# A hybrid decoder layer on one core: value products that begin with the mask made last, and a new written order of the mix's stages

## The chip, the core and the metric

The kernel runs on one core of one Trainium2 chip. The metric is the device time of one execution in microseconds (us). Before the change it is 2168.46 us, the median of 3 runs (2168.17 to 2171.48).

Engine names are those of the profile: PE is the matmul engine, PEld its weight loads, DVE the vector engine, ACT the scalar engine, POOL the GpSimd engine, SP the engine that issues most DMAs.

## What is computed

One decoder layer over 2048 tokens of width 1024, in float32: two head groups side by side (the "mix"), then a gated MLP with a short convolution, then a final norm. Cut to what the change touches:

```python
u = rmsnorm(h, norm_mix_w)
proj = u @ w_in
hq, hf, hi, hg, att = split(proj)
o_hg = hgrn2_chunkwise(q_hg, k_hg, v_hg, log_f)          # 4 heads of 128, recurrent
o_hg = rmsnorm(o_hg, hg_norm_w) * silu(hg)
scores = where(band, q . k / 8, -inf)                    # 8 query heads of 64, 2 key/value heads
m = maximum(max(scores), sink)
p = exp(scores - m)
denom = sum(p) + exp(sink - m)
o_att = (p / denom) . v                                  # own block of 128 keys and the one before
h = h + concat(o_hg, o_att) @ w_out
h = h + (silu(conv(v @ w_gate)) * (v @ w_up)) @ w_down
out = rmsnorm(h, final_norm_w)
```

## The kernel before

The 2048 tokens go through in two halves of 1024. In each half the mix comes first (four recurrent heads in `hgrn`, four pairs of attention heads in `attend`), then the output projection (`out_proj`), the MLP's two up projections (`gate_up`) and its down projection (`down`). Large products are done in a split form: each float32 operand is a rounded part and a rest (`hi`, `lo`), and three matmuls of 512 columns make one product (L202 for the mix's projections).

**Stages.** `hgrn` and `attend` are generators: each `yield` ends a stage. The list `ORDER` names the stages one after the other, and the loop at the end of `hymba_layer` takes them in that order. For head n: `f`, `q` are the forget and query projections, `l` the seven levels of the chunk recurrence, `s` the states, `p` the output, `g` the gate projection, `w` the loading of its weights, `m` a split of a finished piece of the mix. For attention pair n: `qa` is its query projection, `sc` scores and softmax, `pv` and `pw` the value products of the first and the second 512 tokens. `v` is a value projection for two heads. The written order is not the last word: the kernel is built with a scheduler, which places each engine's instructions within their dependences, starting from that written order. What then stands on each engine is shown below, from the built programs.

**Matmuls of the mix, by their line.** L202 projections (results f, hq, q, g and, in `out_proj`, pop); L618 to L620 the value projection (pvv); L387 scores (psc); L423 transposes of the softmax (ppt); L434 value products (poT); L474 diagonal blocks (pdiag); L505 the five fine levels and L519 the two coarse ones (both plev); L552 transposes of K (pkn), L559 state updates (pu), L578 and L580 the head's output (po), L593 its transposes (pot). A row of the trace names the array that a matmul uses: 128\*128 is the whole array. L434 and L474 use half of its columns (128\*64), L519 a quarter or half (128\*32, 128\*64): the result has only 64 or 32 rows. Two products that use different halves of the columns can stand in the array at the same time. A float32 product at full precision (L434, L474, L505, L519, L559, L578, L580) has two records in the trace, a projection or a transpose one.

**The value products.** For each pair and each 512 tokens DVE makes four masked copies of the transposed softmax (L426), in this order: own block for key head 0, previous block for key head 0, own for key head 1, previous for key head 1 (tiles po, pp, po, pp). Then 16 products (L434, 14 at the very start of the sequence, where a block has no previous one) add up in one PSUM bank, poT: for each of four query blocks own and previous mask times V, for key head 0 (lower half of the columns) and key head 1 (upper half).

**Other names.** L512, L522 and L523 multiply Q and K by forget factors (F and a number) between the levels (DVE); L530 puts a level's result into ST (DVE); L404, L405 and L414 belong to the softmax (DVE), the last scales it; L214 splits a finished piece of the mix (DVE); L553 copies transposed K out of PSUM (ACT); L444 and L445 split the last pair's result into XH (ACT) and XL (DVE); L183 and L184 split loaded weights (ACT, DVE). In `hgrn` the flag `late` is set where `ORDER` has head n's `p` ahead of its `g`: then the gate is multiplied in behind the output (L491, L492, L595) and not before (L597).

Of the kernel before, what the change touches and what calls it, by code (L numbers as in the profile page):

```python
# [36 lines left out]
            ("P7", "S3", "T3"), ("P2", "A12", "B21"), ("P4", "A22", "T4")]  # L37
AFTER = {2: 'po'}
UP_AFTER = 'T2'
ORDER = ("f0 q0 l0 qa0 v0 s0 sc0 w0 pv0 p0 f1 q1 l1 g0 pw0 w1 qa1 g1 sc1 f2 s1 q2 p1 qa2 m0 pv1 pw1 l2 v1 "  # L40
         "s2 sc2 f3 m5 q3 g2 p2 pv2 pw2 qa3 m6 m1 sc3 l3 m4 m2 s3 g3 pv3 p3 pw3").split()
LEVELS = [1, 2, 4, 8, 16, 32, 64]
NEG = -1.0e30
UT = 7
# [5 lines left out]
def hymba_layer(ctx: ExitStack, tc: tile.TileContext, a: dict, out: bass.AP, rows_out: bass.AP):  # L50
# [18 lines left out]
    def ps(kind, name):  # L69
        return spaces[kind].tile([P, 512], F32, tag=kind, name=name)  # L70
# [3 lines left out]
    def halves():  # L74
        return [(b, slice(b * 512, (b + 1) * 512)) for b in range(NB)]
# [111 lines left out]
    def unit(src, X, name, order=range(KT), kind="mm", then={}, in_turn=False):  # L187


        hi, lo = src if isinstance(src, tuple) else prep(src)  # L190
        o = [ps(aux[b] if kind == "aux" else kind, f"{name}{b}") for b in range(NB)]
        order = list(order)
        for both in [[h] for h in halves()] if in_turn else [halves()]:
            for i, kt in enumerate(order):
                if i in then:
                    then[i]()
                wh, wl = hi[:, kt * P:(kt + 1) * P], lo[:, kt * P:(kt + 1) * P]
                xh, xl = X[kt]
                for w, x, f, l in ((wh, xh, kt == order[0], False), (wh, xl, False, False),
                                   (wl, xh, False, kt == order[-1])):  # L200
                    for b, bs in both:
                        nc.tensor.matmul(o[b], w, x[:, bs], start=f, stop=l)  # L202
        return o

    def new_x():
        return (xp.tile([P, HALF], F32R, tag="xh", name="XH", bufs=KT),
                xp.tile([P, HALF], F32R, tag="xl", name="XL", bufs=KT))
# [56 lines left out]
    def slot(name):  # L264
        return hp.tile([P, HALF], F32, tag="m", name=name, bufs=KT)
# [47 lines left out]
    def blocks(t, turn=False):  # L313

        v = t.rearrange("p (g r) -> p g r", r=32)
        return v[:, :, ::-1] if turn else v
# [6 lines left out]
    def rows(kv):  # L323
        return slice(kv * HD, (kv + 1) * HD)
# [32 lines left out]
    def attend(hf, j, X, invb, KS, V, mix, p):  # L357

        o = unit(a["w_att"][j], X, "q")
        qT = slot(f"att{j}")  # L360
        for b, bs in halves():
            nc.vector.scalar_tensor_tensor(blocks(qT[:, bs], b), blocks(o[b]), 0.125, blocks(invb[:, bs]),
                                           op0=ALU.mult, op1=ALU.mult)
            nc.scalar.activation(qT[:, bs], qT[:, bs], AF.Identity, bias=C.bq[:, j:j + 1])
        yield
        scs = []
        for g in range(NB):
            sc = p.tile([P, 2, 4, P], F32, tag="sc", name="sc", bufs=2)
            gs = slice(g * 512, (g + 1) * 512)
            for kv in range(2):  # L370
                r, other = rows(kv), rows(1 - kv)

                qh, ql = [p.tile([P, 512], F32R, tag="pp", name=n, bufs=4) for n in ("qh", "ql")]
                nc.scalar.copy(qh[r], qT[r, gs])
                nc.scalar.copy(qh[other], qT[r, gs])
                nc.vector.tensor_tensor(ql[r], qT[r, gs], qh[r].bitcast(F32), op=ALU.subtract)
                nc.scalar.copy(ql[other], ql[r].bitcast(F32))
                for i0 in (0, 2):
                    pb = ps("at", "psc")
                    first = hf == 0 and g == 0 and i0 == 0  # L380
                    for i in range(2):
                        n = g * 4 + i0 + i
                        w0 = 1 if first and i == 0 else 0
                        o = pb[:, i * 256 + w0 * P:(i + 1) * 256]
                        ks = slice((n + w0) * P, (n + 2) * P)
                        for t, qx in enumerate((qh, ql)):
                            nc.tensor.matmul(o, qx[:, (i0 + i) * P:(i0 + i + 1) * P], KS[:, kv, ks],  # L387
                                             start=t == 0, stop=t == 1)
                    pv = pb.rearrange("p (i w k) -> p i w k", i=2, w=2)
                    dst = sc[:, kv, i0:i0 + 2]  # L390
                    if first:
                        nc.vector.memset(dst[:, 0], NEG)
                        nc.scalar.copy(dst[:, 1], pv[:, 1, 0])
                    else:
                        nc.scalar.copy(dst, pv[:, :, 0])
                    nc.vector.copy_predicated(
                        dst, C.own.bitcast(U32).unsqueeze(1).to_broadcast([P, 2, P]), pv[:, :, 1])
            m = p.tile([P, 2, 4], F32, tag="mx", name="m", bufs=2)
            nc.vector.tensor_reduce(m.rearrange("p a b -> p (a b)"),
                                    sc.rearrange("p a b c -> p (a b) c"), axis=AX.X, op=ALU.max)  # L400
            sk = C.sinkb[:, j].unsqueeze(2).to_broadcast([P, 2, 4])
            nc.vector.tensor_tensor(m, m, sk, op=ALU.max)
            es = p.tile([P, 2, 4], F32, tag="es", name="es", bufs=2)
            nc.vector.tensor_tensor(es, sk, m, op=ALU.subtract)  # L404
            nc.vector.tensor_scalar(m, m, -1.0, None, op0=ALU.mult)  # L405
            den = p.tile([P, 2, 4], F32, tag="den", name="den", bufs=2)
            for kv in range(2):
                for i in range(4):
                    nc.scalar.activation(sc[:, kv, i], sc[:, kv, i], AF.Exp, bias=m[:, kv, i:i + 1],
                                         accum_out=den[:, kv, i:i + 1])  # L410
            nc.scalar.activation(es, es, AF.Exp)
            nc.vector.tensor_tensor(den, den, es, op=ALU.add)
            nc.vector.reciprocal(den, den)
            nc.vector.tensor_tensor(sc, sc, den.unsqueeze(3).to_broadcast([P, 2, 4, P]), op=ALU.mult)  # L414
            scs.append(sc)
        yield
        for g, sc in enumerate(scs):
            pm = []
            for kv in range(2):
                pm.append([p.tile([P, 4, P], F32, tag="pp", name=n, bufs=4) for n in ("po", "pp")])  # L420
                pt = ps("at", "ppt")
                for i in range(4):
                    nc.tensor.transpose(pt[:, i * P:(i + 1) * P], sc[:, kv, i], ident)  # L423
                ptv = pt.rearrange("p (i q) -> p i q", i=4)
                for dst, mk in zip(pm[kv], (C.ownT, C.prevT)):
                    nc.vector.tensor_tensor(dst, ptv, mk.unsqueeze(1).to_broadcast([P, 4, P]), op=ALU.mult)  # L426
            oT = ps("at", "poT")
            for i in range(4):
                n = g * 4 + i
                noprev = hf == 0 and n == 0  # L430
                for prev in range(1 if noprev else 2):
                    for kv in range(2):
                        r = rows(kv)
                        nc.tensor.matmul(oT[r, i * P:(i + 1) * P], V[:, n + 1 - prev, r], pm[kv][prev][:, i],  # L434
                                         start=prev == 0, stop=noprev or prev == 1)
            gs = slice(g * 512, (g + 1) * 512)
            if j < ATT_J - 1:
                nc.scalar.copy(qT[:, gs], oT)
                mix[4 + j] = qT
            else:  # L440
                if g == 0:
                    mix[4 + j] = new_x()
                h, l = mix[4 + j]
                nc.scalar.copy(h[:, gs], oT)  # L444
                nc.vector.tensor_tensor(l[:, gs], oT, h[:, gs].bitcast(F32), op=ALU.subtract)  # L445
            yield

    def hgrn(hf, h, X, invb, vs, WG, gates, mix, p, fu=None):
# [31 lines left out]

        late = ORDER.index(f"p{h}") < ORDER.index(f"g{h}")

# [605 lines left out]
    kv = [first_unit(X, W, i) for i in range(2)]  # L1088
    constants()
    xs.inverse("x")  # L1090
    f0 = unit(a["w_f"][0], X, "f", kind="aux", then={4: xs.spread})
    nxt = X, kv, xs.acc, xs.rs, f0
    for hf in range(NH):
        X, kv, invb, rs, f0 = nxt
        with ExitStack() as st:
# [6 lines left out]
            pairs = [attend(hf, h, X, invb, KS, V, mix, p) for h in range(HG)]  # L1102
            for name in ORDER:
                stage, n = name[:-1], int(name[-1])
# [87 lines left out]
```

## Time and profile before

| What | us |
|---|---|
| median of 3 runs | 2168.46 |
| the profiled execution, its own time | 2167.45 |
| span of the profiled execution (first to last instruction) | 2165.7 |
| mix of the first half, from the first attention projection to the unbroken run of the output projection | 46.7 to 397.0 of the span |
| mix of the second half | 1124.0 to 1471.0 |
| ACT busy in the span | 1046.9 (48%) |
| DVE busy in the span | 1624.0 (75%) |

The span is 1.75 us shorter than the profiled execution's own time, which counts what lies before the first and after the last instruction. The rows of the trace give start and length of each instruction in us from the start of the span. Matmuls overlap: a row of 512 columns lasts 0.39 us, but the next starts 0.23 us later. So the time that a piece of work takes on PE is read from the distance between starts, not from the lengths. In the timeline a row with x2 is two records that follow each other, and its length reaches from the start of the first to the end of the last.

### The profile page before, as it was taken

To read this page: it belongs to the slowest core of one execution; us is meant where nothing else is said; L and a number is where in the kernel's file an instruction comes from. 1 tells how busy PE (TensorE), PEld (TensorE's weight loads), DVE (VectorE), ACT (ScalarE), POOL (GpSimd) and SP (SyncE) were. 2 spreads that over 40 slices of the span, in tenths; PEclk is the share of its full clock that TensorE was granted. 3 is DMA by queue.
4 is the path that set the end of the run, shared out by engine and by line. 5 is a ranking of instruction groups with operands and counts; after the bars stand their busy time and mean duration, and the time that the engine had idled before them with its cause. 6 is when DMAs were issued, how large, how long until landed. Compare 5 with 4: busy or idle time off the path is not lost.

```text
span 2165.7 us, 29275 instructions
## 1 busy us (share of the span) xinstructions
PE 2148.0 (99%) x11319; PEld 1801.6 (83%) x11319; DVE 1624.0 (75%) x2429; ACT 1046.9 (48%) x1836; POOL 20.7 (1%) x45
## 2 busy tenths in 40 slices
PE   8999999999999999999999999999999999999998
PEld 7988988888888888888889889888888888888887
DVE  6676668689787888785765666677888888787865
ACT  6445455454444445345635355445544444444453
POOL 3000000000000000000000000000000000000000
PEclk9999999999999999999999999999999999999999
DMA  4101012413232234964641111114232423259743
GB/s 157 40 30 39 30 40 69 136 59 127 93 114 96 92 127 147 378 242 150 210 136 31 30 49 31 50 54 149 70 112 88 132 83 123 87 187 396 237 146 132
DMA packets 91148, 254.43 MB, mean 117 GB/s; under 512 B 11136, under 2 KB 13952, under 8 KB 91008
## 3 DMA queue, kind: packets, MB, share of 16 engines
q1 hardware_dynamic: 90576, 252.29, 34.9%
q8 instruction: 89, 1.46, 0.3%
q14 instruction: 51, 0.42, 0.1%
q10 hardware_dynamic: 432, 0.27, 0.0%
HBM read 195.37 MB, written 57.15 MB: 117 GB/s over the span
## 4 chain that ended last, share of the span: by engine, by line
PE 97%; DVE 2%; DMA 0%; ACT 0%; issue 0%; SPq 0%; DVEq 0%; ACTq 0%
PE X L751 7%; PE X L753 7%; PE X L752 7%; PE pop L202 7%; PE q L202 4%; PE g L202 4%; PE hq L202 4%; PE f L202 4%; PE Y L753 4%; PE Y L752 4%; PE Y L751 4%; PE pdx L938 3%; PE pdx L939 3%; PE pdx L940 3%; PE pdy L939 3%; PE pdy L940 3%
## 5 line engine op out<-in xcount | busy, mean ns | idle before, releaser
L626 ACT CAST whi<-raw 128x1024 fp32r<-128x1024 f32 x88 | 92.5, 1051 | 102.4 <-PE X L752 68.3
L822 DVE SCALAR_TENSOR_TENSOR y<-ga,cw,y 128x1024 f32<-128x1024 f32 x88 | 112.2, 1277 | 37.7 <-ACT y L820 37.7
L751 PE MATMUL X<-T,whi 128*128 128x512 f32 x352 | 136.9, 389 | 0.0
L752 PE MATMUL X<-T,whi 128*128 128x512 f32 x352 | 136.9, 389 | 0.0
L753 PE MATMUL X<-T,wlo 128*128 128x512 f32 x352 | 136.9, 389 | 0.0
L627 DVE TENSOR_TENSOR wlo<-raw,whi 128x1024 fp32r<-128x1024 f32 x88 | 107.1, 1217 | 5.6 <-ACT whi L626 5.6
L183 ACT CAST whi<-raw 128x1024 fp32r<-128x1024 f32 x58 | 60.5, 1048 | 102.5 <-PE q L202 22.3
L757 ACT COPY u<-X 128x512 f32<-128x512 f32 x88 | 51.7, 587 | 99.8 <-PE X L753 99.8
L627 DVE TENSOR_TENSOR xld<-raw,xhd 128x1024 fp32r<-128x1024 f32 x72 | 80.8, 1129 | 8.8 <-ACT xhd L626 8.6
L626 ACT CAST xhd<-raw 128x1024 fp32r<-128x1024 f32 x72 | 69.3, 978 | 34.9 <-DMA raw<-act0B 10.6
L202 PE MATMUL pop<-XL,whi 128*128 128x512 f32 x256 | 84.2, 392 | 0.0
L202 PE MATMUL pop<-XH,wlo 128*128 128x512 f32 x256 | 83.3, 390 | 0.8 <-DVE wlo L184 0.8
L202 PE MATMUL pop<-XH,whi 128*128 128x512 f32 x256 | 83.4, 396 | 0.5 <-ACT XH L444 0.2
L184 DVE TENSOR_TENSOR wlo<-raw,whi 128x1024 fp32r<-128x1024 f32 x58 | 70.1, 1213 | 13.4 <-ACT whi L183 13.4
L753 PEld LDWEIGHTS X<-T,wlo 128*128 128x128 f32 x352 | 66.1, 188 | 13.7
L752 PEld LDWEIGHTS X<-T,whi 128*128 128x128 f32 x352 | 66.1, 188 | 13.7
L751 PEld LDWEIGHTS X<-T,whi 128*128 128x128 f32 x352 | 66.1, 188 | 13.7
L757 ACT COPY s<-X 128x512 f32<-128x512 f32 x44 | 25.9, 588 | 106.4 <-PE X L753 106.4
L618 PE MATMUL pvv<-whi,XH 128*128 128x256 f32 x256 | 73.0, 286 | 0.0
L619 PE MATMUL pvv<-whi,XL 128*128 128x256 f32 x256 | 72.9, 286 | 0.0
L620 PE MATMUL pvv<-wlo,XH 128*128 128x256 f32 x256 | 72.8, 288 | 0.0
L751 PE MATMUL X<-T,Sh 128*128 128x512 f32 x176 | 68.7, 390 | 0.0
(393 smaller groups left out, 6508.6 us busy)
## 6 DMA issues: line engine op xcount, KB each, us to landing
wr<-in_w_down SPq DMA_DIRECT2D x90, 512.0 KB, 5.6
raw<-in_w_gate SPq DMA_DIRECT2D x44, 512.0 KB, 3.6
raw<-in_w_up SPq DMA_DIRECT2D x44, 512.0 KB, 3.6
raw<-act0T SPq DMA_DIRECT2D x20, 512.0 KB, 5.5
raw<-act1T SPq DMA_DIRECT2D x20, 512.0 KB, 5.1
act0B<-y SPq DMA_DIRECT2D x33, 256.0 KB, 2.3
act1B<-y SPq DMA_DIRECT2D x33, 256.0 KB, 2.2
raw<-in_w_out SPq DMA_DIRECT2D x16, 512.0 KB, 3.7
```

The lines of the kernel that those rows point to most:

```text
L202: nc.tensor.matmul(o[b], w, x[:, bs], start=f, stop=l)
L618: nc.tensor.matmul(o[:, 0:256], xh[:, t], hi[:, c], start=kt == 0, stop=False)
L619: nc.tensor.matmul(o[:, 0:256], xl[:, t], hi[:, c], start=False, stop=False)
L626: nc.scalar.copy(h, src)
L627: return (eng or nc.vector).tensor_tensor(l, src, h.bitcast(F32), op=ALU.subtract)
L751: nc.tensor.matmul(o, wh[:, ws], xh, start=i == 0 and not more, stop=False, skip_group_check=more)
L752: nc.tensor.matmul(o, wh[:, ws], xl, start=False, stop=False, skip_group_check=more)
L753: nc.tensor.matmul(o, wl[:, ws], xh, start=False, stop=i == 3, skip_group_check=more)
L757: nc.scalar.copy(t, o)
L822: nc.vector.scalar_tensor_tensor(y, g[:, w:w + HALF], C.cw[:, ft, w:w + 1], y, op0=ALU.mult, op1=ALU.add)
L939: nc.tensor.matmul(o, wh[:, i, c], al[:, i, cols], start=False, stop=False, skip_group_check=more)
L940: nc.tensor.matmul(o, wl[:, i, c], ah[:, i, cols], start=False, stop=l, skip_group_check=more)
```

## The change

Two edits. The first turns the order of the sixteen value products of a bank round: in each query block the previous mask comes before the own one, and key head 1 before key head 0. The first product so reads the mask that DVE makes last (the tile pp of key head 1; in the first query block of the sequence, which has no previous block, po of key head 1). The flags that start and end an accumulation move along. The second is another list `ORDER`; as head 2's `p` now stands ahead of its `g`, `late` holds for head 2 as well as for head 0.

```diff
-ORDER = ("f0 q0 l0 qa0 v0 s0 sc0 w0 pv0 p0 f1 q1 l1 g0 pw0 w1 qa1 g1 sc1 f2 s1 q2 p1 qa2 m0 pv1 pw1 l2 v1 "
-         "s2 sc2 f3 m5 q3 g2 p2 pv2 pw2 qa3 m6 m1 sc3 l3 m4 m2 s3 g3 pv3 p3 pw3").split()
+ORDER = ("f0 q0 l0 qa0 v0 s0 f1 p0 sc0 w0 pv0 q1 l1 qa1 pw0 g0 s1 qa2 sc1 w1 m4 f2 pv1 g1 p1 m1 q2 pw1 l2 "
+         "sc2 v1 m0 pv2 qa3 s2 p2 pw2 f3 m6 q3 l3 m5 sc3 g2 pv3 pw3 m2 g3 s3 p3").split()
...
                 noprev = hf == 0 and n == 0
-                for prev in range(1 if noprev else 2):
-                    for kv in range(2):
+                for prev in (0,) if noprev else (1, 0):
+                    for kv in (1, 0):
                         r = rows(kv)
                         nc.tensor.matmul(oT[r, i * P:(i + 1) * P], V[:, n + 1 - prev, r], pm[kv][prev][:, i],
-                                         start=prev == 0, stop=noprev or prev == 1)
+                                         start=noprev or prev == 1, stop=prev == 0)
```

The built programs hold the same 10359 matmuls of the same sizes. On PE the order differs from the first half's second head to the first pieces of `out_proj`, and likewise in the second half; `gate_up` and `down` stand as before.

**First place: PE, the first bank of value products of the first half.** Before, it lies in the query projection of head 1 (hq):

```order
L202 MATMUL hq_1270<-XL,whi 128x512
L202 MATMUL hq_1271<-XL,whi 128x512
L434 MATMUL poT<-po,V 64x128
L202 MATMUL hq_1270<-XH,wlo 128x512
L434 MATMUL poT<-po,V 64x128 x3
L434 MATMUL poT<-pp,V 64x128 x2
L434 MATMUL poT<-po,V 64x128 x2
L434 MATMUL poT<-pp,V 64x128 x2
L434 MATMUL poT<-po,V 64x128 x2
L434 MATMUL poT<-pp,V 64x128 x2
L202 MATMUL hq_1271<-XH,wlo 128x512
```

Now it lies in the query projection of attention pair 1 (q), and head 1's diagonal blocks follow it:

```order
L202 MATMUL q_1453<-XH,whi 128x512
L434 MATMUL poT<-po,V 64x128 x2
L434 MATMUL poT<-pp,V 64x128 x2
L434 MATMUL poT<-po,V 64x128 x2
L434 MATMUL poT<-pp,V 64x128 x2
L434 MATMUL poT<-po,V 64x128 x2
L434 MATMUL poT<-pp,V 64x128 x2
L434 MATMUL poT<-po,V 64x128 x2
L474 MATMUL pdiag<-hg_1320,K 64x64 x16
L505 MATMUL plev<-Q,G 128x2x64 x4
```

The single product ahead of one hq matmul is gone; all 14 stand together, in pairs, and run into another piece of half-array work.

**Second place: PE, near the end of the first half's mix.** Before, the last pair's first bank lies between the coarse levels of head 3, behind its own transposes (ppt):

```order
L505 MATMUL plev<-Q,G 128x2x64 x4
L423 MATMUL ppt<-ident,sc 128x128 x8
L519 MATMUL plev<-Q,K 32x32 x16
L434 MATMUL poT<-po,V 64x128 x4
L434 MATMUL poT<-pp,V 64x128 x2
L434 MATMUL poT<-po,V 64x128 x2
L434 MATMUL poT<-pp,V 64x128 x2
L434 MATMUL poT<-po,V 64x128 x2
L434 MATMUL poT<-pp,V 64x128 x2
L519 MATMUL plev<-Q,K 64x64 x8
```

Now that bank stands between the two last fine levels; the later half of its transposes lies 24 matmuls of the output projection and one level further up, the earlier half above that (not shown):

```order
L505 MATMUL plev<-Q,G 128x2x64 x4
L434 MATMUL poT<-po,V 64x128 x2
L434 MATMUL poT<-pp,V 64x128 x2
L434 MATMUL poT<-po,V 64x128 x2
L434 MATMUL poT<-pp,V 64x128 x2
L434 MATMUL poT<-po,V 64x128 x2
L434 MATMUL poT<-pp,V 64x128 x2
L434 MATMUL poT<-po,V 64x128 x2
L505 MATMUL plev<-Q,G 128x2x64 x4
L202 MATMUL pop_3543<-XH,whi 128x512
L202 MATMUL pop_3544<-XH,whi 128x512
L202 MATMUL pop_3612<-XH,whi 128x512
```

One more projection matmul and then the coarse level (L519) follow; the last coarse level comes 24 projection matmuls after that one.

**Third place: DVE, beside the second.** Before, the four masks stand between the multiplications for the last fine level and those for the coarse ones:

```order
L512 TENSOR_TENSOR Q<-Q,F_3219 128x2x16x16
L530 COPY_PREDICATED ST<-lmask_313,plev 128x2x16x16
L426 TENSOR_TENSOR po<-ppt,ownT 128x512
L426 TENSOR_TENSOR pp<-ppt,prevT 128x512
L426 TENSOR_TENSOR po<-ppt,ownT 128x512
L426 TENSOR_TENSOR pp<-ppt,prevT 128x512
L522 TENSOR_TENSOR Q<-Q,F_3231 128x16x32
L523 TENSOR_TENSOR K<-K,F_3231 128x16x32
```

Now the masks of that bank are made earlier, and the bank's split (L445) stands ahead of the last fine level's multiplication (the second L512), which the coarse level reads:

```order
L512 TENSOR_TENSOR Q<-Q,F_3022 128x2x32x8
L530 COPY_PREDICATED ST<-lmask_307,plev 128x2x32x8
L404 TENSOR_TENSOR es<-sinkb,m 128x8
L445 TENSOR_TENSOR XL<-poT,XH 128x512
L405 TENSOR_SCALAR m<-m 128x8
L512 TENSOR_TENSOR Q<-Q,F_3034 128x2x16x16
L530 COPY_PREDICATED ST<-lmask_313,plev 128x2x16x16
L214 TENSOR_TENSOR XL<-hg_2099,XH 128x1024
L522 TENSOR_TENSOR Q<-Q,F_3046 128x16x32
L523 TENSOR_TENSOR K<-K,F_3046 128x16x32
```

So L445 moved from behind the coarse level's multiplications to ahead of the last fine level's, and the masks moved away from that place.

## The prediction

> **What bounds the kernel now.** I read the page first: busy shares, granted clock, and the chain that ended last.
>
> ```profile
> span 2165.7 us, 29275 instructions
> PE 2148.0 (99%) x11319; PEld 1801.6 (83%) x11319; DVE 1624.0 (75%) x2429; ACT 1046.9 (48%) x1836; POOL 20.7 (1%) x45
> PEclk9999999999999999999999999999999999999999
> PE 97%; DVE 2%; DMA 0%; ACT 0%; issue 0%; SPq 0%; DVEq 0%; ACTq 0%
> ```
>
> PE is busy for 99% of the span at a full clock, and the chain runs over it for 97%. Whatever PE is spared shortens the kernel, as long as no other engine takes its place. The change rearranges the mix alone, so next I took windows over the two mixes (columns: length, then busy us and instructions of PE, PEld, DVE, ACT, POOL, then granted clock, DMA share, GB/s).
>
> ```profile
> 46.70:397.00 350.30, 348.20 (x2421) 299.25 (x2420) 237.74 (x453) 175.38 (x438) 1.57 (x3) 1.00 0.15 44
> 1124.00:1471.00 347.00, 344.67 (x2414) 297.27 (x2412) 228.83 (x430) 171.27 (x432) 1.56 (x3) 1.00 0.15 44
> ```
>
> In 350 us PE rests for 2, DVE works for 238 (68%), ACT for 175, and DMA stands at a share of 0.15. Matmul lengths overlap, though, so "busy" hides slow stretches. What a matmul costs is the distance between starts. A long unbroken run gives the pace (a line of the chain in order of time: start, length, what):
>
> ```profile
> 286.63 10.88 PE g L202 x48
> ```
>
> 10.88 / 48 = 0.227 us for a projection matmul. Now the stretch in which the first bank of value products lies, in the timeline of PE (start, length, instruction):
>
> ```profile
> 128.47 0.61 PE L202 MATMUL hq<-XL,whi 128*128 128x512 f32 x2
> 129.02 0.43 PE L434 MATMUL poT<-po,V 128*64 128x128 f32 x2
> 129.38 0.49 PE L202 MATMUL hq<-XH,wlo 128*128 128x512 f32 x1
> 129.80 0.54 PE L434 MATMUL poT<-po,V 128*64 128x128 f32 x5
> ...
> 130.19 0.38 PE L434 MATMUL poT<-pp,V 128*64 128x128 f32 x2
> ...
> 130.63 0.38 PE L434 MATMUL poT<-pp,V 128*64 128x128 f32 x2
> ...
> 131.48 0.50 PE L202 MATMUL hq<-XH,wlo 128*128 128x512 f32 x1
> 131.81 0.63 PE L202 MATMUL hq<-XH,whi 128*128 128x512 f32 x2
> ```
>
> Inside, from 130.19 to 130.63, four products pass in 0.44 us: 0.11 each, with both halves of the columns at work. The edges cost extra. Going in: two hq matmuls from 128.47 would end their turn at 128.92, poT starts at 129.02, so 0.10. Coming out: from 131.48 to 131.81 is 0.33 where the pace is 0.23, so another 0.10. The 13 products from 129.80 to 131.48 take 1.68 us where 13 x 0.109 = 1.42, so 0.26 more, in which the first products, the last and the odd one with half the array idle are slow. Sum for this stretch: **0.46**. The lone product takes 0.36 (129.02 to 129.38), where in company it takes 0.11: with both edges **0.45**, for one product.
>
> The whole kernel has 63 stretches of half-array work. For each I took the distance of starts across it less its matmuls at their paces, each overlap counted once; the first and the last of the 63:
>
> ```profile
> 61.40 1.15 PE L474 MATMUL pdiag<-hg,K 128*64 128x64 f32 x32
> ...
> 1446.29 0.48 PE L434 MATMUL poT<-pp,V 128*64 128x128 f32 x3
> ```
>
> The surplus is 29.8 us in all: 27 stretches with an even number of products 9.2 (0.34 each), 16 with an odd number 6.6 (0.41), 18 lone products 8.5 (0.47), and 2 that hold waits as well 5.5. That is what the change can touch.
>
> **The change part by part.** *Fewer stretches.* The order of PE now has 37 stretches, all even, none lone: 33 of one kind of work and 4 of two kinds (two banks of value products with diagonal blocks, two with a coarse level inside). At 0.34, and 0.40 for a mixed one, they cost 33 x 0.34 + 4 x 0.40 = 12.8 us. Of the two waiting stretches' 5.5, some 0.9 are edges (0.45 each). So the edges fall from 24.3 + 0.9 = 25.2 to 12.8: **-12.4 us**. It holds only where PE is the bound, which it is on 97% of the chain.
>
> The Trainium skill, page "TensorEngine Tiling (Array Packing)", section "Key Properties", says that a change of tiling mode drains the engine, and that tiles work side by side. The trace agrees with both (0.10 at the way in; 0.36 for a lone product against 0.11). Taken as the two drains alone, about 0.19 a stretch, the rule would give 26 x 0.19 = 4.9 us, and leave out the idle half and the slow second start.
>
> *Waits that go.* The two mixed stretches lie near each mix's end. That of the first half:
>
> ```profile
> 359.49 0.70 PE L519 MATMUL plev<-Q,K 128*32 128x32 f32 x32
> 361.37 1.05 PE L434 MATMUL poT<-po,V 128*64 128x128 f32 x7 [1.18 <-DVE pp L426]
> 363.67 0.69 PE L519 MATMUL plev<-Q,K 128*64 128x64 f32 x16
> ```
>
> ```profile
> 359.95 0.68 DVE L426 TENSOR_TENSOR po<-ppt,ownT 128x512 f32<-128x512 f32 x1
> 360.54 0.68 DVE L426 TENSOR_TENSOR pp<-ppt,prevT 128x512 f32<-128x512 f32 x1
> 361.14 0.68 DVE L426 TENSOR_TENSOR po<-ppt,ownT 128x512 f32<-128x512 f32 x1
> 361.74 0.68 DVE L426 TENSOR_TENSOR pp<-ppt,prevT 128x512 f32<-128x512 f32 x1
> ```
>
> PE reaches the value products while DVE makes their masks, 0.60 apart, and waits. In the new order 24 output projections (24 x 0.227 = 5.4 us) and a level lie between transposes and products, against some 2.5 us for four masks: these waits, 5.5 - 0.9, go: **-4.6 us**.
>
> *What is late next.* Three places at each mix's end become tight. First, the coarse level behind the moved bank reads what the second L512 makes, and ahead of that on DVE now stands L445, behind ACT's L444:
>
> ```profile
> L444 ACT CAST XH<-poT 128x512 fp32r<-128x512 f32 x4 | 2.3, 586 | 11.5 <-PE poT L434 11.5
> L445 DVE TENSOR_TENSOR XL<-poT,XH 128x512 fp32r<-128x512 f32 x4 | 2.7, 687 | 0.9 <-ACT XH L444 0.9
> L512 DVE TENSOR_TENSOR Q<-Q,F 128x512 f32<-128x512 f32 x32 | 22.0, 687 | 31.4 <-PE plev L505 31.4
> ```
>
> From the bank's end that chain is 0.59 + 0.69 + 0.17 (a small one) + 0.69 and some 0.2 of handing over, 2.3 us; PE has a level (8 records x 0.112), four projections (0.91) and edges of 0.3 to do, 2.1: 0.2 of waiting. Second, transposed K (L552) follows the last level after 8 transposes and 2 projections, 1.3 us; L522 and L523 need as much: 0 to 0.2. Third, the state updates now follow L552 at once, and before they had a lone product between:
>
> ```profile
> 367.26 1.04 PE L552 MATMUL pkn<-ident,K 128*128 128x128 f32 x8
> 368.33 0.40 PE L434 MATMUL poT<-po,V 128*64 128x128 f32 x2
> 368.67 1.16 PE L559 MATMUL pu<-v,Kn 128*128 128x128 f32 x8
> ```
>
> 368.67 - 368.33 = 0.34 were covered; uncovered, with ACT's copy (L553) between, about 0.4. Together 0.8 a half: **+1.6 us**, between nothing and the 4.6 removed.
>
> *Waits elsewhere.* The scores of pair 2 now all lie beside head 2's levels, by the count of its rows the stretch in which DVE is packed tightest, and weight splits (L184) stand behind them. In the first half the gate of head 1 starts about 1.7 us after the projection whose weight buffer it takes, for a cast and a difference:
>
> ```profile
> L183 ACT CAST whi<-raw 128x1024 fp32r<-128x1024 f32 x58 | 60.5, 1048 | 102.5 <-PE q L202 22.3 <-issue 16.3 <-PE pop L202 14.2
> L184 DVE TENSOR_TENSOR wlo<-raw,whi 128x1024 fp32r<-128x1024 f32 x58 | 70.1, 1213 | 13.4 <-ACT whi L183 13.4
> ```
>
> The third matmul needs the difference, at 1.05 + 1.21 plus handing over, 0.3 later than PE comes. The trace of before cannot show such places. The low end is a gain of 0.6: PE's rest in the first window is 2.1 us, and 1.2 of it is the wait counted above, so some 0.3 a half is left to lose. The high end is +5: two places a half at which PE waits for a whole cast and difference (1.05 + 1.21). I take **+0.8**, near the low end, since the row nearest to these places, PE's rest, is small.
>
> *What costs nothing.* The turned order by itself adds no matmul. `late` for head 2 trades 4 DVE rows for 4 others and adds 4 ACT rows, under 3 us on an engine idle half the mix. SP issues the same weight loads in another order; they wait for buffers, and DMA stands at a share of 0.15. POOL keeps its order. If that cover is gone, PE waits for one load (the page's list of DMA issues: 3.7 us to landing):
>
> ```profile
> raw<-in_w_out SPq DMA_DIRECT2D x16, 512.0 KB, 3.7
> ```
>
> Sum: -12.4 - 4.6 + 1.6 + 0.8 = **-14.6 us**, 2167.45 - 14.6 = 2152.9 for the profiled execution. The median is 1.0 higher, so 2153.9.
>
> **The rivals.** *A: DVE becomes the bound.* The new order packs DVE tighter than I see, and 5 to 12 of the 17 us come back as waits (2157 to 2164). For it: from 355 to 370 DVE is busy for 14.3 of 15 us,
>
> ```profile
> 355.00:370.00 15.00, 13.43 (x141) 10.71 (x139) 14.30 (x27) 6.41 (x24) 0.00 (x0) 1.00 0.00 1
> ```
>
> against it: the same work at each end is spread further now.
>
> *B: the last mask is waited for everywhere (slower).* All 16 products of a bank now stand behind the mask made last, 3 x 0.60 = 1.8 us after the first. Matmuls behind them wait too. If DVE is late at each of the 16 banks, that is up to 28.8 us against 17 saved, 2180; from 10 banks on the kernel is slower. 12 banks would give 2173. Against it: in the new order, by its rows at their paces, 4 to 9 us of PE work lie between a bank's last transpose and its first product at 14 banks, and 2.8 and 3.1 at the last of each half, against 2.5 for masks. That matmuls start in program order is also what the Trainium skill says, page "TensorE: Matmul & The Clock Gate", section "The mechanism"; here the wait at 361.37, with L519 queued behind, agrees.
>
> *C: it does not do what it says.* Edges are saved, but PE then stands at the same DVE results as before: within 0.2% of 2168. The 97% of the chain on PE speaks against it.
>
> **How the numbers follow.** Forecast 0.75 (2150 to 2157), A 0.16, C 0.06, B 0.03. Nothing above 17 us is to be had: 2168.5 - 17.0 = 2151.5, less 1.5 for the surplus of edges being read a little small: low end 2150. The high end takes in A's greater part, 2162. A measurement of this kernel can tell about 0.2% (4.3 us) from no change, so faster means below 2164.1: forecast and nearly all of A, 0.90; within 0.2%: C and A's rest, 0.07; slower 0.03.
>
> **What would show it.** Right: 37 stretches of half-array work with some 13 us of surplus, no lone value product, no wait at L434 above 0.3 us. The mixes 7 us shorter each, gate_up and down unchanged. Wrong: waits at L434 for L426 (B); gaps of PE at levels, L559 or projections for DVE or weights in the middle of the mix (A); edges that cost as much in sum as before (C).

## The result, and the profile after

Over four runs each on one chip the changed kernel takes 2157.81 us (2156.57 to 2160.39), the kernel before 2169.97 (2168.17 to 2172.4): a ratio of 0.9946, 95% interval 0.993 to 0.9961. The gain is 12.2 us; 14.6 were forecast. Two later executions at a lower granted clock, one of order_only (2377.84 us, 0.85) and one of split_pool (2907.67 us, 0.69), count in no ratio below. The profiled execution of the changed kernel took 2158.96. Its page:

```profile
span 2157.2 us, 29283 instructions
PE 2138.4 (99%) x11319; PEld 1797.8 (83%) x11319; DVE 1622.0 (75%) x2429; ACT 1054.6 (49%) x1844; POOL 17.0 (1%) x45
PE 95%; DVE 3%; ACT 1%; issue 0%; DMA 0%; SPq 0%; DVEq 0%; ACTq 0%
```

PE does the same 11319 matmuls and is still busy for 99%, but 5% of the chain now lies elsewhere, mostly on DVE. To see where, I cut each mix in two: the **middle**, from the first diagonal block of head 0 to that of head 3, and the **end**, from there to the last row of head 3's output (L580). Windows of the kernel before (length, busy us of PE, PEld, DVE, ACT, POOL, then granted clock, DMA share, GB/s), middle and end of the first mix, then of the second:

```profile
61.40:326.61 265.21, 265.21 (x1882) 230.69 (x1882) 172.42 (x333) 132.66 (x335) 1.57 (x3) 1.00 0.12 35
326.61:378.23 51.62, 50.03 (x390) 42.47 (x389) 42.30 (x74) 30.20 (x85) 0.00 (x0) 1.00 0.23 73
1134.95:1400.69 265.74, 265.74 (x1890) 231.42 (x1889) 170.59 (x321) 133.31 (x335) 1.56 (x3) 1.00 0.12 35
1400.69:1452.19 51.50, 49.68 (x393) 42.77 (x393) 41.09 (x72) 30.24 (x85) 0.00 (x0) 1.00 0.25 78
```

The same four windows after, and between the mixes the one that holds gate_up and down (686.35 us before):

```profile
62.45:321.25 258.80, 258.80 (x1891) 229.72 (x1890) 171.44 (x337) 138.81 (x356) 1.56 (x3) 1.00 0.11 34
321.25:373.56 52.31, 50.23 (x382) 41.49 (x382) 42.69 (x69) 26.66 (x68) 0.00 (x0) 1.00 0.26 81
443.89:1131.84 687.95, 687.95 (x3068) 569.95 (x3066) 546.07 (x713) 321.60 (x432) 0.52 (x1) 1.00 0.45 153
1131.84:1391.22 259.38, 259.38 (x1899) 229.70 (x1898) 167.98 (x325) 139.56 (x355) 1.56 (x3) 1.00 0.11 34
1391.22:1443.75 52.53, 50.40 (x386) 41.78 (x386) 42.36 (x68) 26.90 (x69) 0.00 (x0) 1.00 0.27 86
```

The middles are 6.4 us shorter each, the ends 0.7 and 1.0 longer: 5.7 and 5.3 a mix, 11.1 in all, where 7 each were forecast. The boundary shifts a little work between the two, so below I compare their **surplus**, reckoned as in the prediction: the distance of starts less the matmuls at their paces.

A bank in the middle now, from PE's timeline (start, length, instruction):

```profile
142.67 0.40 PE L202 MATMUL q<-XH,whi 128*128 128x512 f32 x1
143.00 0.44 PE L434 MATMUL poT<-po,V 128*64 128x128 f32 x4
143.27 0.39 PE L434 MATMUL poT<-pp,V 128*64 128x128 f32 x4
...
144.58 1.10 PE L474 MATMUL pdiag<-hg,K 128*64 128x64 f32 x32
```

The products begin behind the projection and run on into the diagonal block, in one stretch without a lone product. There are 37 stretches, as the order of rows said. They cost 14.3 us of surplus, against 29.8. Four near the ends hold 2.0 of waits, so the edges cost 12.4 (12.8 forecast): 0.29 to 0.36 a clean one.

What PE waits for in the changed kernel (us in total, times, longest):

```profile
PE kv L202 <- ACT XH L216: 6.4, 2, 6.1
PE pop L202 <- DVE wlo L184: 1.5, 4, 0.4
PE pop L202 <- DVE XL L214: 0.9, 2, 0.6
PE pu L559 <- ACT Kn L553: 0.6, 2, 0.3
PE ppt L423 <- DVE sc L396: 0.6, 2, 0.3
PE pop L202 <- ACT XH L213: 0.5, 1, 0.5
...
PE plev L505 <- DVE Q L512: 0.4, 1, 0.4
PE poT L434 <- DVE pp L426: 0.3, 1, 0.3
```

The first row is the kernel's start, as before. In the list of before, pop waits for L184 twice, 0.8 in all, and poT stands with

```profile
PE poT L434 <- DVE pp L426: 2.5, 3, 1.2
```

Of the rows that are new after the change, all lie in the ends. One of them, in PE's timeline:

```profile
351.68 1.13 PE L505 MATMUL plev<-Q,G 128*128 128x128 f32 x8 [0.44 <-DVE Q L512]
354.00 0.70 PE L519 MATMUL plev<-Q,K 128*32 128x32 f32 x32
355.33 0.73 PE L202 MATMUL pop<-XL,whi 128*128 128x512 f32 x2 [0.63 <-DVE XL L214]
```

and the window over DVE's part of that end:

```profile
324.35:357.30 32.95, 31.13 (x205) 25.08 (x204) 32.05 (x47) 18.13 (x37) 0.00 (x0) 1.00 0.38 117
```

DVE works for 32.05 of 32.95 us there. Five differences of the mix's split (L214, 1.22 us each) stand in it one soon after another, since by the program they take buffers of X, which the last gate projection has to read first (no row shows a wait for these buffers). So the question for the experiments: does DVE's backlog bring the 17 us down to 11, and what does each half of the change do alone?

### The profile page after: what moved, and what is told of

The parts are those of the page before. It is cut to its first block, busy times and chain, and to the rows that moved or that the text cites. A ratio compares the mean times of both kernels' runs of the same rounds, so it can differ in the third digit from the quotient of the medians.

```text
span 2157.2 us, 29283 instructions
## 1 busy us (share of the span) xinstructions
PE 2138.4 (99%) x11319; PEld 1797.8 (83%) x11319; DVE 1622.0 (75%) x2429; ACT 1054.6 (49%) x1844; POOL 17.0 (1%) x45
## 4 chain that ended last, share of the span: by engine, by line
PE 95%; DVE 3%; ACT 1%; issue 0%; DMA 0%; SPq 0%; DVEq 0%; ACTq 0%
PE X L751 7%; PE X L753 7%; PE X L752 7%; PE pop L202 7%; PE f L202 4%; PE q L202 4%; PE hq L202 4%; PE Y L751 4%; PE Y L753 4%; PE Y L752 4%; PE pdx L938 3%; PE pdx L940 3%; PE pdx L939 3%; PE g L202 3%; PE pdy L940 3%; PE pdy L938 3%
## 5 line engine op out<-in xcount | busy, mean ns | idle before, releaser
L184 DVE TENSOR_TENSOR wlo<-raw,whi 128x1024 fp32r<-128x1024 f32 x58 | 70.3, 1216 | 11.7 <-ACT whi L183 11.7
```

## Experiments

All are held against the kernel before on the same chip. The surplus is in us, both mixes together; "middles" and "ends" count everything above the paces, half-clock stretches too. The surplus of order_only is read from order_again, the same kernel; that of split_pool was not worked out.

| kernel | median us | ratio (95%) | stretches in the middles | middles | ends |
|---|---|---|---|---|---|
| before | 2169.1 to 2170.0 | 1 | 50 | 21.8 | 12.1 |
| after_again | 2157.52 | 0.9946 (0.9934 to 0.9959) | 27 | 10.8 | 12.0 |
| order_only | 2170.55 | 1.0003 (0.9993 to 1.0012) | 37 | 17.0 | 21.1 |
| mask_only | 2171.35 | 1.0009 (1.0 to 1.0018) | 36 | 14.4 | 22.5 |
| tail_new | 2171.39 | 1.0011 (1.0002 to 1.002) | 37 | 17.1 | 17.8 |
| tail_old | 2160.82 | 0.996 (0.9947 to 0.9974) | 27 | 10.8 | 15.7 |
| split_pool2 | 2162.71 | 0.997 (0.9959 to 0.9982) | 27 | 10.8 | 18.0 |
| split_pool | 2174.0 | 1.0023 (1.0013 to 1.0032) | - | - | - |
| split_act | 2155.51 | 0.9936 (0.9922 to 0.9949) | 27 | 10.8 | 10.0 |
| no_low | 2157.18 | 0.9941 (0.9928 to 0.9955) | 27 | 10.8 | 10.9 |
| unpaired | 2158.44 | 0.9951 (0.9937 to 0.9965) | 27 | 11.8 | 12.1 |
| heads_apart | 2183.09 | 1.0065 (1.0051 to 1.0078) | 30 | 27.8 | 19.9 |

**The changed kernel again** (after_again, no edit).

> The changed kernel once more, on the chip of these runs: 2156 to 2160 by the four runs so far. Its half-array stretches cost 14.3 us again (12.4 of it edges) and TensorE waits 3.2 to 3.3 us a half at the mixes' ends. If the half-clock stretch behind the one-column matmuls at 1088.6 belongs to this kernel it is there again; if it comes and goes, the time lies near 2156.6 where it is missing and near 2159 to 2160 where it is there.

2157.52 us (2156.55 to 2159.04). The profiled execution, 2156.55, has the stretches' 14.3 us and the ends of the first one, and no half-clock stretch near 1088: the window between the mixes lasts 686.24 instead of 687.95. So that stretch comes and goes, and costs 1.7.

**Each half of the change alone.** order_only takes the new ORDER and leaves the products as they were; mask_only the reverse.

```diff
 order_only, against the changed kernel
-                for prev in (0,) if noprev else (1, 0):
-                    for kv in (1, 0):
+                for prev in range(1 if noprev else 2):
+                    for kv in range(2):
...
 mask_only, against the changed kernel
-ORDER = ("f0 q0 l0 qa0 v0 s0 f1 p0 ...
+ORDER = ("f0 q0 l0 qa0 v0 s0 sc0 w0 pv0 ...
```

> The new written order of the stages, with the value products in their old order (own mask's product first). TensorE's row order is that of the changed kernel but for these products: 49 half-array stretches instead of 37, 12 of them a lone value product, 14 with an odd number. Theory 1, the edges are paid at their price: at 0.34 an even stretch, 0.41 an odd and 0.47 a lone one (rows of the kernel before) the stretches cost 23 x 0.34 + 14 x 0.41 + 12 x 0.47 = 19.2 us against 12.4 measured in the changed kernel, so 6.8 us more than it: 2164 to 2165. Rival, TensorE would have stood for VectorE at these places anyhow (VectorE bounds the mixes' ends): within 2 us of the changed kernel, 2156 to 2160.

> The old written order of the stages, with the value products begun by the mask made last. 47 half-array stretches instead of the 63 before, 2 of them lone, 2 odd. Theory 1: edges of 43 x 0.34 + 2 x 0.41 + 2 x 0.47 = 16.4 us against 24.3 before (without the two mixed stretches that wait), -7.9. The bank that stood mixed with the level now stands whole behind its last transpose with only a level of 64 between: it waits for two masks, about 1 us a half, against 2.3 a half before. Sum -7.9 - 2.6 = -10.5: 2158 to 2161. Rival B of the prediction, every bank waits for its last mask: each of 16 banks 0.6 to 1.8 us at the value products, 2168 and more.

> The new written order with the old product order once more, for a profile at full clock (its timed runs gave 2170.5, the profiled one had a clock of 0.85). It is 13 us slower than the changed kernel where 6.8 were expected. If only the edges are dearer, its stretches cost some 25 us and the waits between whole-array matmuls are those of the changed kernel, 16 us. If the old product order makes new waits (a lone first product holds its bank and what is queued behind it until the second mask is there), they show as waits at the value products or behind them, some 6 us, at the mixes' ends.

Both expectations failed: neither half gains anything by itself. In order_only the scheduler had also replanned the middle, so "but for these products" was too much said. order_again is the same kernel as order_only once more (one run, 2172.82), and its trace is the one read here. Edges are saved in both: the middles lose 4.8 us of surplus in order_only and 7.4 in mask_only. The ends take it back, with 9 to 10 us more than before. In order_again, PE's timeline in the first end:

```profile
344.54 0.66 PE L423 MATMUL ppt<-ident,sc 128*128 128x128 f32 x4
346.40 0.40 PE L434 MATMUL poT<-po,V 128*64 128x128 f32 x2 [1.20 <-DVE pp L426]
347.00 0.47 PE L202 MATMUL pop<-XH,whi 128*128 128x512 f32 x1 [0.20 <-DVE hg L488]
...
348.64 1.02 PE L202 MATMUL pop<-XH,wlo 128*128 128x512 f32 x2 [0.39 <-DVE wlo L184]
349.45 1.05 PE L202 MATMUL pop<-XH,whi 128*128 128x512 f32 x2
```

```profile
345.00:348.50 3.50, 1.85 (x8) 0.79 (x6) 3.50 (x6) 1.79 (x3) 0.00 (x0) 1.00 0.12 46
...
349.00:352.40 3.40, 3.40 (x10) 2.64 (x9) 3.40 (x6) 1.90 (x2) 0.00 (x0) 0.51 0.51 154
```

A lone product stands right behind the transposes and waits 1.20 for DVE's masks, the projections queued behind it wait too, and PE is busy for 1.85 of 3.5 us. Then two projections start 0.86 apart instead of 0.45: the granted clock is 0.51 for 3.4 us. Three such stretches lie in this kernel's ends, some 4 to 5 us. In mask_only it is the whole bank that stands close behind its transposes, and waits for the masks of key head 1, the two that DVE makes last:

```profile
359.49 0.69 PE L519 MATMUL plev<-Q,K 128*64 128x64 f32 x16 [1.72 <-DVE K L523]
361.21 0.70 PE L434 MATMUL poT<-po,V 128*64 128x128 f32 x4 [1.04 <-DVE po L426]
...
367.33 1.08 PE L202 MATMUL pop<-XH,whi 128*128 128x512 f32 x2 [1.87 <-ACT XH L444]
```

This is rival B at one bank a mix, in small: the bank waits 1.0 in the first end and 1.3 in the second, of the 10 us by which the ends grew. The rest stands around it: 1.72 and 1.3 for what the coarse level ahead reads (L523, L512), 1.87 and 1.0 for L444 behind, and three half-clock stretches (0.50 from 360.69 to 364.10, from 367.51 to 370.92 and from 1439.30 to 1442.71). That the new product order pays only where the written order puts work between transposes and products fits this, but was not tested by itself.

The Trainium skill, page "TensorE: Matmul & The Clock Gate", section "What's actually happening", has the clock fall to half after an idle window of about 3.4 us and stay there for a busy one. The length agrees. The condition does not: no gap here is longer than 2 us. The busy share of the profile does not part the cases either: PE was busy for 1.91 of the 3.41 us ahead of the drop in order_again (345.49 to 348.90), and for 1.68 of 3.41 in the second end of tail_new (1431.25 to 1434.66), where the clock held. The work does, nearly. All changes of the clock within one execution lie whole multiples of 3.41 us apart (348.90, 1424.10, 1437.75 in order_again). On that grid, with each matmul counted at its pace and a one-column one as nothing, the 14 windows ahead of a drop, over the traces of 13 executions, hold 0.7 to 1.36 us of matmuls, and the windows at full clock with none behind them 1.25 or more (1.25 in the mixed stretch of the second mix of before). That is a count from these traces; no run varied the work by itself.

**Which of it is the ends, which the middle.** The product order depends on the pair: pair 3 stands at the ends.

```diff
 tail_new, against the changed kernel (tail_old: j < ATT_J - 1)
+                noprev, new = hf == 0 and n == 0, j == ATT_J - 1
-                for prev in (0,) if noprev else (1, 0):
-                    for kv in (1, 0):
+                for prev in (0,) if noprev else (1, 0) if new else (0, 1):
+                    for kv in (1, 0) if new else (0, 1):
...
```

> The new written order; pair 3, whose value products stand at the mixes' ends, has the new product order, pairs 0 to 2 the old one. 45 half-array stretches, 11 with an odd number and 9 lone. Theory G, order_only lost its gain mostly at the two mixes' ends (a lone product that waits 1.9 us for its second mask there, then stretches of 3.4 us at half the clock): here only edges are left, 25 x 0.34 + 11 x 0.41 + 9 x 0.47 = 17.2 us against 12.4, so 4.8 us above the changed kernel, 2161 to 2163. Rival H, each lone product costs about 1.1 us wherever it stands (13 us by 12): 9 of them, 2166 to 2168.

> The complement of tail_new: pairs 0 to 2 have the new product order, pair 3 the old one. 39 stretches, 3 odd and 3 lone, so 1.5 us of edges more than the changed kernel. Theory G: the lone product behind the transposes at a mix's end waits 1.5 us and what follows costs half-clock stretches of some 1.7 us each: 2162 to 2167, with granted clock 0.5 for 3.4 us behind a value product at least once. Rival H: 3 x 1.1 us, 2160 to 2161, at full clock through both mixes' ends.

tail_new was to get back most of order_only's loss and did not: 2171.39 (2168.7 to 2176.53), above both theories. tail_old took 2160.82, the number of H, at full clock. The surplus tells more than either theory. Against the changed kernel tail_new has 6.3 more in the middles (4.8 expected) and 5.8 more in the ends, though the products there are in the new order; tail_old has nothing in the middles and 3.7 in the ends. That 5.8 and 3.7 come near the 9.1 of order_only says little, since the ends of these kernels are not the same rows in the same order. PE in tail_new's first end:

```profile
355.27 1.16 PE L505 MATMUL plev<-Q,G 128*128 128x128 f32 x8
357.35 0.70 PE L519 MATMUL plev<-Q,K 128*32 128x32 f32 x32 [0.92 <-DVE Q L512]
359.53 1.13 PE L519 MATMUL plev<-Q,K 128*64 128x64 f32 x16 [1.49 <-DVE den L412]
```

In the changed kernel 4 projections stand between the last fine level and the first coarse one, and 24 between the two coarse ones. Here, in both ends, there are none, and both coarse levels wait for DVE, 0.9 and 1.5; from 359.47 to 362.88 the clock is 0.50. Further up, in both ends, the projections behind the first transposes wait 1.8 for L488, which DVE now does behind two masks (at 345.46; the masks at 344.26 and 344.86) and in the changed kernel ahead of them (341.32; 343.64). The second end of order_again has the coarse levels without projections between them and the same waits (0.9 and 1.5). In tail_old's first end no projection is left between the rows of the output, and L578 waits there 0.5 four times for ACT (L581). So an edit of the products in the middle, or of pair 3 alone, makes the scheduler plan an *end* anew, and the new waits stand where that plan differs. G was wrong in taking the ends for something that pair 3's products alone decide. What the product order costs with the rest of the order held fixed was not run.

**DVE's backlog.** First I moved differences of the split to GpSimd, two of six (split_pool2) or all.

```diff
 split_pool2 (split_pool: eng=nc.gpsimd)
-                    M[n] = split(mix[n])
+                    M[n] = split(mix[n], eng=nc.gpsimd if n in (0, 1) else None)
```

> The changed kernel with 2 of the 6 differences a half that split the mix (pieces of heads 0 and 1) made by GpSimd instead of VectorE, which then has 2 x 1.22 us less a half in the stretch before the last levels. Theory D, the 6.5 us of new waits of TensorE at the mixes' ends come of VectorE's backlog there: TensorE's waits at the transposes, the second projection's weights, the level's Q and the late split shrink by 2 to 3 us a half, the sum of surplus between whole-array matmuls goes from 16 to 10 to 12 us, and the time to 2152 to 2154. Rival E, the waits come of the tail's own order (a chain from level to level with too little beside it): they stay within 1 us a half and the time within 2 us of the changed kernel. GpSimd's price for a 128 x 1024 difference is in no row yet; up to 5 us each nothing should wait for it, since the projections take these pieces some 5 us apart.

> The changed kernel with all 6 differences a half on GpSimd: VectorE has 7.3 us less a half. Theory D: no TensorE wait for VectorE above 0.2 us is left before the last levels; 2151 to 2154, if a difference on GpSimd takes no more than about 2 us. Rival E: within 2 us of the changed kernel. Third outcome: GpSimd is slow enough (over 2.5 us each, 15 us a half) that the projections wait for it: slower than the changed kernel, with GpSimd as the releaser of those waits.

Slower by 5 and 16 us, which neither D nor E had; the third outcome, with another cause. POOL and then DVE in split_pool2:

```profile
326.35 5.95 POOL L214 TENSOR_TENSOR XL<-hg,XH 128x1024 fp32r<-128x1024 f32 x2 [20.72 <-ACT XH L213]
```

```profile
326.62 3.43 DVE L184 TENSOR_TENSOR wlo<-raw,whi 128x1024 fp32r<-128x1024 f32 x1
330.09 0.45 DVE L396 COPY_PREDICATED sc<-own,psc 128x256 f32<-128x256 uint32 x1
330.43 2.41 DVE L512 TENSOR_TENSOR Q<-Q,f 128x512 f32<-128x512 f32 x1
```

While POOL makes two differences (3.0 each), DVE's weight difference takes 3.43 instead of 1.22, and L512 2.41 instead of 0.69. DVE is rid of 2.4 us and loses 3.9. The Trainium skill, page "GPSIMD Engine Reference", section "1. Specifications", says that the two share their SBUF interfaces and contend where a DVE instruction has two SBUF inputs; the trace agrees.

So I took the work away without POOL. Both kernels leave out part of the computation: split_act copies the piece on ACT as the low part for heads 0 and 1; no_low leaves out all six low parts a half, and the projections read the high part twice.

```diff
 split_act (eng=n in (0, 1)); no_low: eng=True, and l = h in place of the copy
-            (eng or nc.vector).tensor_tensor(l, src, h.bitcast(F32), op=ALU.subtract)
+            nc.scalar.copy(l, src) if eng else nc.vector.tensor_tensor(l, src, h.bitcast(F32), op=ALU.subtract)
```

> The changed kernel; for pieces of heads 0 and 1 the low part of the split is left out (ScalarE copies the piece in its place), so VectorE has 2 x 1.22 us less a half in the stretch before the last levels, ScalarE 2 x 1.05 more, and GpSimd has nothing. The run with GpSimd was 5 us slower, which leaves two readings. Theory D, VectorE's backlog sets TensorE's waits at the mixes' ends (GpSimd slowed VectorE itself: a weight difference of 3.43 instead of 1.22 us stood beside it): here the waits shrink by 2 to 3 us a half, to 2152 to 2154. Rival E, the tail's own order sets them: within 2 us of the changed kernel, 2156 to 2160. Rival F, ScalarE is as late as VectorE: waits move from VectorE to ScalarE as releaser, same time.

> The changed kernel with all 6 low parts a half of the mix's split left out (the projections read the high part in their place): VectorE has 6 x 1.22 = 7.3 us less a half in front of the last levels, and no other engine has more. TensorE's work is the same; 37 stretches, one of them lone. From the first product of head 3's diagonal to the last row of its output the changed kernel takes 52.3 and 52.5 us, some 3.5 of it waits. Theory D, VectorE's backlog sets these waits: 49 to 50 us, and 2151 to 2153 in all. Rival E, the chain of levels, masks and state updates sets them whatever else VectorE has to do (moving a third of the differences to ScalarE gave 1.0 us a half): 51 to 52 us, 2155 to 2157.

split_act: 2155.51, the ends 1.0 and 1.1 us shorter; nearer E than D. no_low: 2157.18, nothing that can be told from the changed kernel, and this is E's end of the range. Its two ends:

```profile
321.30:373.36 52.06, 49.25 (x381) 42.03 (x381) 36.23 (x63) 26.72 (x69) 0.00 (x0) 1.00 0.26 82
1391.20:1442.83 51.63, 50.41 (x386) 42.18 (x385) 35.80 (x62) 26.97 (x70) 0.00 (x0) 1.00 0.27 88
```

DVE works 6.5 us less in each end (36.23 against 42.69), and the end is 0.25 and 0.9 shorter. What PE waits for in the first one:

```profile
PE po L578 <- ACT on L581: 1.0, 2, 0.5
PE pkn L552 <- ACT XH L444: 0.8, 1, 0.8
PE po L578 <- DVE SS L566: 0.7, 1, 0.7
PE ppt L423 <- DVE sc L414: 0.3, 1, 0.3
```

Of the changed kernel's waits in this end none is left, and others stand in their place, farther down head 3's chain: bank to L444 to L552, states to output, output to its squares. With less on DVE, PE waits *elsewhere* in the end, and hardly less. The scheduler planned the ends of both kernels anew (in no_low the projections are used up earlier), so this is not the same order with less to do, and it does not measure what the backlog costs in the changed kernel's order; an order held fixed was not tried.

**The price of half an array.** What does a lone product cost beside its edges? Two orders in which products of one half of the array stand in a row, two or eight:

```diff
 unpaired
-                for prev in (0,) if noprev else (1, 0):
-                    for kv in (1, 0):
+                for kv in (1, 0):
+                    for prev in (0,) if noprev else (1, 0):
 heads_apart
-            for i in range(4):
+            for kv, i in [(kv, i) for kv in (1, 0) for i in range(4)]:
...
```

> The changed kernel with each token block's value products in the order head 1 previous, head 1 own, head 0 previous, head 0 own, so that products of the two halves of the array stand side by side only every other time. In the changed kernel four records (two products, one of each half) take 0.22 us, 1.74 us a bank of 16 products. Theory 1, two products go side by side only where neighbours use different halves of the array: a neighbour of the same half costs a full slot; of 15 neighbouring pairs in a bank 15 differ in half now, 7 then, so some 8 x 0.11 = 0.9 us a bank, 14 us in all: 2170 to 2174. Rival, the pace belongs to the half-array shape itself: no change, 2156 to 2160.

> The changed kernel with all 8 value products of head 1 of a bank ahead of the 8 of head 0 (39 stretches, 3 of them lone: 1.5 us of edges). unpaired, with two products of a head in a row, cost only 0.05 us a bank, against what was expected of it. Theory Q1, TensorE starts records in program order and lays a few of the other half beside them: with 8 products in a row most of the overlap is gone, up to 1.7 us a bank, over 16 banks 20 us and more, 2178 to 2184. Theory Q2, the two halves of the array take their own records independently through a whole bank: 2159 to 2161.

unpaired costs 0.9 us in all (0.05 a bank), not 14; heads_apart 25.6 over the changed kernel, as Q1 said. A bank of heads_apart in PE's timeline:

```profile
162.38 0.43 PE L434 MATMUL poT<-pp,V 128*64 128x128 f32 x2
...
163.52 0.38 PE L434 MATMUL poT<-po,V 128*64 128x128 f32 x2
163.74 0.44 PE L434 MATMUL poT<-pp,V 128*64 128x128 f32 x4
163.96 0.44 PE L434 MATMUL poT<-po,V 128*64 128x128 f32 x4
164.23 0.38 PE L434 MATMUL poT<-pp,V 128*64 128x128 f32 x2
...
165.32 0.38 PE L434 MATMUL poT<-po,V 128*64 128x128 f32 x2
165.64 0.73 PE L202 MATMUL q<-XH,wlo 128*128 128x512 f32 x2
```

A row of x2 is one product and takes 0.22; a row of x4 is two, one in each half, and takes 0.22 as well. Twelve products pass alone and four in company: 3.26 us, against 1.90 for a bank of the changed kernel, so 12 x 0.11 more. With two in a row the second of one head and the first of the next still go together, and nothing is lost but at the last. This is the idle half that the prediction put beside the edges of an odd stretch.

## Why the prediction was right, and which step was mis-sized

Direction, range and mechanism held: half-array stretches became fewer at the price that was read for them, and the waits at the mixed stretches went. The forecast's own band, 2150 to 2157, was missed by 0.8 us; 2157.81 lies at the low end of rival A's (2157 to 2164). By its steps, in us of surplus (before and after_again):

| step | forecast | measured |
|---|---|---|
| fewer stretches | -12.4 | -12.8 (25.2 to 12.4) |
| waits at the two mixed stretches go | -4.6 | -4.6 |
| what is late next, at the mixes' ends | +1.6 | **+6.8** |
| waits elsewhere | +0.8 | -0.5 |
| sum | -14.6 | -11.1 |

- **Fewer stretches.** Right in number and price. The four stretches of two kinds cost 0.34 to 0.35 each, not 0.40.
- **Waits that go.** poT waits 0.3 us for a mask, once.
- **What is late next.** This step is the one that was mis-sized. Of its three places, L552 (0.17 over its pace) and L559 (0.40 and 0.51) came as worked out. The coarse level behind the bank, for which 0.2 stood, does not wait for the second L512; the fine level ahead of it waits 0.44 for an L512, in the first mix alone. Left out were other places of the same end: the transposes that wait for a bank that L396 has yet to read (0.45 over the pace in each mix), the projection that waits for L184 (0.57 in each), those that wait for the last split (0.7 in the first mix, 0.7 and 0.4 in the second). These come to 3.8 us; the step was short by 5.2. I had followed the chain behind the moved bank only. I had set nothing against the end as a whole: before, it had 12.1 us of surplus, after it has 12.0.
- **Waits elsewhere.** None shows in the middles, where the prediction put them; rows other than stretches have 0.5 less surplus there than before. That this step erred by 1.3 the other way brought the sum nearer, and was luck.
- **Rival A** had the right size at its low end (5 of the 17 come back). Its row lay in the end, where the waits are; its sign, gaps in the middle of the mix, is not seen. Its cause, DVE as the bound, is borne out only in part: most of the new waits are for DVE, but taking 7.3 us a half from it returned 1.1 of the 6.8 and taking 2.4 returned 2.0, each with the ends planned anew.
- **Rival B** is not seen in the changed kernel. mask_only shows it for a bank close behind its transposes, at 1.0 and 1.3 us. The program order of starts on which B rests holds at its row (361.37), but not always between the two halves of the array (last section).
- **Rival C**'s outcome, edges saved and the time unchanged, is what each half of the change gives alone. The two together gain.

The medians differ by 12.2 and the traces by 11.1 in the mixes. The profiled execution of before (2167.45) was quicker than its median by 1.0 to 2.5, and half-clock stretches of 1.7 us come and go (one in the first profiled execution of the changed kernel, none in the second or in that of before; the timed runs of before lie between granted clocks of 0.997 and 1.0). The rest is within what these move, which is not to say that they are its cause.

What sets the length of the ends stays open: with less on DVE they were 1 to 2 of their 12 us shorter, in another order. No version that computes everything beat the changed kernel.

## What to carry to other kernels

Price each change of the array's shape by its stretch (here 0.34 us, and 0.11 more for a product whose other half has no work), and count the stretches from the order of rows: that sum came out to within 4%. Where a stage ends in a chain of dependent steps, take its surplus as a whole and ask how much of it the change can touch at all; a wait that goes there is replaced by the next one along the chain. Test the halves of a two-part change alone before believing either: here each was worth nothing, and both 12 us. Where a scheduler places the rows, compare the built orders before putting a difference down to the edited lines: here edits in the middle had the end planned anew, and in tail_new the ends took 5.8 us more.

## What the runs showed of the hardware, unexpected

- A wait of 1.2 to 2 us can cost 1.7 more: the granted clock fell to 0.5 for 3.41 us (order_again, mask_only, tail_new, split_pool) where the matmuls of the 3.41 us ahead came to 0.7 to 1.36 us at their paces, on a grid of 3.41 us; windows with 1.25 and more held it. Waits of 0.4 to 0.7 in the changed kernel's ends did not bring it down. The stretch behind one-column matmuls (L243) fits: the window ahead of it (1085.19 to 1088.60) holds 24 of them and some four projections, 0.9 us, and it comes and goes between executions of one kernel.
- Products of the two halves of the array go side by side with two of the same half in a row, at the full pace of 0.11 each. In heads_apart, by the names in the rows, the first product of head 0 starts beside the seventh of head 1 (163.75 and 163.74) and ahead of the eighth (163.96), which the built program has ahead of it: half-array matmuls do not always start in program order.
- A difference of 128 x 1024 takes POOL 2.4 to 3.4 us (DVE 1.22), and two of DVE's two-input instructions beside it took 3.43 instead of 1.22 and 2.41 instead of 0.69.
